# Dilated attention in a two-block network: scores in a PSUM place of their own, gate products held between blocks, bias tiles made a group ahead

## The chip, the cores and the metric

The kernel runs on one core of a Trainium2 chip. The metric is the device time of one execution in microseconds. TensorE (matrix products), VectorE, ScalarE, GpSimd and the DMA queues work side by side; each runs its own instructions in a fixed order, and they wait for each other by semaphores. The order is laid down when the program is built: the builder goes through the traced instructions and gives each engine, among those that are ready by its own estimate, the one that it ranks first. A note "issue after X" adds an edge in issue order only: the instruction is put behind X on X's engine, with no wait for X to end.

## The reference, cut to what matters

A first block (gated linear recurrence, window attention, convolution GLU) feeds a second block, which normalises x to xn and runs four mixers on a projection of it: pooling, dilated attention, stick-breaking attention and a state space layer (S5). Each mixer's output is projected and multiplied with its own gate, and the sum goes on to a feed-forward layer:

```python
for bi, yb in enumerate((y_pool, y_dil, y_sb, y_s5)):
    gate = jax.nn.sigmoid(xn @ w_gate[l, bi])
    merged = merged + gate * (yb @ w_branch[l, row:row + width])
```

The gates hang on xn alone, so they can be computed at any time after the norm. The change is about dilated attention. Twelve heads of 64 stand in three groups of four, with dilations 1, 4 and 16. A group's queries see the keys of their band, with a relative bias by a table:

```python
s = jnp.einsum('bdhnqe,bdhnke->bdhnqk', qb, kb) / math.sqrt(E)
s = jnp.where(mask, s + bias, -1e30)
m = jnp.max(s, axis=-1, keepdims=True)
p = jnp.exp(s - m)
den = jnp.sum(p, axis=-1, keepdims=True)
o = jnp.einsum('bdhnqk,bdhnke->bdhnqe', p, vb) / den
lse = (m + jnp.log(den))[..., 0]
```

The three groups' outputs are then weighed by a softmax over their `lse`. The sequence has 1024 tokens, the model width is 1024, everything is float32.

## The kernel before

Second block, in program order: stick-breaking attention (`stick`, L1737), dilated attention (`dilated`, L1838), S5 (L2028), merge (L2377). Wide products are split in a high and a low part, hi·hi + lo·hi + hi·lo, which is three matmuls for one (`gemm`, L354).

**Gates.** 32 gate tiles (four mixers by eight column tiles of 128) are to be made. `fill` (L304) takes the next one off a list: `gate` (L2359) loads 512 KB of weights, splits them (ScalarE and VectorE, L386 and L387), runs the product against the split xn (8 row tiles, 3 products, 2 halves: 48 matmuls of 512 columns, L362, L364, L366) in a PSUM tile of two banks, lets ScalarE write the tanh to `gf`, and stores that to memory as `gd`. `fill` stands at chosen places of the mixers, so that TensorE has work while a mixer's chain waits: six gates in `stick`, in `dilated` after blocks 1, 4 and 6 of each group (`FILL`, L40) and one after the third group's statistics, sixteen in S5. Only that last one of `dilated` is held by an edge (L1965); the others may be put wherever the builder finds them ready.

**PSUM.** There are eight banks. Two tiles of two banks each, `mm0` and `mm1`, are handed out in turn by `pmm` (L288), or by number. Four tiles of one bank, `ax`, come from `pax` (L292).

**Dilated attention, per group** (L1853). First the bias: one-hot tables are loaded, a small product with the bias table gives four rows (L1860), a mask is added (L1861), the rows are stored to memory (L1862) and loaded back four times as a Toeplitz tile `hk`, two buffers (L1867); a product with a reversed identity turns each (L1869), and VectorE copies it out as `bias` (L1871). Then the values: group 0 makes them by a projection (L1886), groups 1 and 2 load a transposed form and turn it with TensorE (`turn`, L1900, L1902), between the loads of q and k (L1908). Then eight blocks of 128 queries (L1913):

1. scores, four heads in two `ax` tiles (L1926). A block that sees its predecessor's keys is "wide" (256 keys), the others are "narrow" (128): group 0 has one narrow block (0), group 1 narrow blocks at even places, group 2 only narrow ones;
2. VectorE adds the bias and takes the maximum of each head (L1929), and negates it (L1932);
3. ScalarE takes the exponentials and their sums, a head at a time (L1934);
4. TensorE transposes them, four heads to an `ax` tile (L1939); ScalarE and VectorE copy them out (L1942, L1944);
5. the values product in one `ax` tile (L1951), copied to the group's result (L1954, L1956).

After the blocks, maxima and sums are transposed (L1963) and, for groups 1 and 2, reordered through memory (L1973, L1979). After the third group, the weights of the groups are computed on VectorE and ScalarE, spread (L2007, L2018) and applied (L2019, L2021).

Of the kernel before, what the change touches and what calls it, by code (L numbers as in the profile page):

```python
# [9 lines left out]
F32 = mybir.dt.float32  # L10
# [8 lines left out]
P = 128  # L19
D = 1024  # L20
T = 1024
HT = 512
# [237 lines left out]
class Kern:  # L260
# [40 lines left out]
        return self.smalls[:, o + j : o + j + 1]  # L301


    def fill(self, fp, bufs=1, turn=None, raw=False):  # L304
        if self.todo:
            b, m = self.todo.pop(0)
            g = fp.tile([P, T], F32, tag="gf", name=self.nm("gf"), bufs=bufs) if fp else self.big("gf")
            self.gate(g, b, m, turn, raw)
            if raw:
                self.raw.add((b, m))  # L310
            self.gd[b, m] = self.spill("gd", g)
# [1526 lines left out]
    def dilated(self):  # L1838
        nc, tc, A = self.nc, self.tc, self.A
        ID = self.c("ident")  # L1840
        out = []
        with tc.tile_pool(name="dl", bufs=1) as fp:
# [7 lines left out]
            ED = self.dp.tile([12, 384], F32, name=self.nm("ED"), tag="ED")  # L1850
            SD = self.dp.tile([3, 2, 32, P], F32, name=self.nm("SD"), tag="SD")
            num, stat = [], []
            for g, dil in enumerate((1, 4, 8)):  # L1853

                oh = fp.tile([32, 384], F32, tag="oh", name=self.nm("oh"))
                ng = fp.tile([4, 384], F32, tag="ng", name=self.nm("ng"))
                nc.sync.dma_start(oh, A["dil_oh"][g])
# [5 lines left out]
                bias = []  # L1863
                for h in range(4):
                    hk = fp.tile([P, 256], F32, tag="hk", name=self.nm("hk"), bufs=2)
                    e = ED[4 * g + h, :]
                    nc.sync.dma_start(hk, bass.AP(e.tensor, e.offset, [[1, P], [1, 256]]))  # L1867
                    pb = self.pax(256)
                    nc.tensor.matmul(pb, lhsT=self.c("rev"), rhs=hk, start=True, stop=True)  # L1869
                    t = fp.tile([P, 256], F32, tag="bias", name=self.nm("bias"), bufs=4)  # L1870
                    nc.vector.tensor_copy(t, pb)  # L1871
                    bias.append(t)
                if g == 0:
                    nat = lambda x, n: x[:, n * P : (n + 1) * P]
                elif g == 1:
                    nat = lambda x, n: x[:, (n % 2) * 512 + n // 2 : (n % 2) * 512 + 512 : 4]
                else:
                    nat = lambda x, n: x[:, n:T:8]
# [9 lines left out]
                else:  # L1888

                    for m in range(2):  # L1890
                        t = self.big("dvf")
# [3 lines left out]
                def turn(m):  # L1895
                    for i in range(2):
                        pp = self.pax()
                        for b in range(4):
                            c = (4 * i + b) * P
                            nc.tensor.transpose(pp[:, b * P : (b + 1) * P], vf[m][:, c : c + P], ID)  # L1900
                        o = vt[i].rearrange("p (b c) -> p b c", b=4)[:, :, m * P : (m + 1) * P]
                        nc.vector.tensor_copy(o, pp.rearrange("p (b c) -> p b c", b=4))  # L1902


                q, k = [], []
                for m in range(4):
                    t = self.big("dq" if m < 2 else "dk")
                    nc.sync.dma_start(t, self.dqd[4 * g + m])  # L1908
                    (q if m < 2 else k).append(t)
                    if vf and m in (1, 2):  # L1910
                        turn(m - 1)
                nt = [fp.tile([P, T], F32, name=self.nm("num")), self.big("num")]
                for n in range(8):  # L1913
                    prev = n > 0 if g == 0 else (n % 2 == 1 if g == 1 else False)
                    k0, c0 = ((n - 1) * P, 0) if prev else (n * P, P)
                    W = 256 - c0
                    sl = slice(n * P, (n + 1) * P)
                    s4 = fp.tile([P, 4, 256], F32, tag="ds", name=self.nm("ds"), bufs=2)
                    m4, d4 = mst[:, g, 0, :, n], mst[:, g, 1, :, n]
                    nm = self.small(4, "nm")  # L1920

                    pr = [self.pax(), self.pax()]
                    for j in range(2):
                        for r in range(2):
                            hp = slice(64 * r, 64 * r + 64)
                            nc.tensor.matmul(pr[r][:, j * 256 : j * 256 + W], lhsT=q[j][hp, sl], rhs=k[j][hp, k0 : (n + 1) * P], start=True, stop=True)  # L1926
                    for h in range(4):
                        j, r = divmod(h, 2)
                        nc.vector.tensor_tensor_reduce(  # L1929
                            s4[:, h, c0:256], pr[r][:, j * 256 : j * 256 + W], bias[h][:, c0:256], 1.0, -3e38, ALU.add, ALU.max, m4[:, h : h + 1]  # L1930
                        )
                    nc.vector.tensor_scalar(nm, m4, -1.0, None, ALU.mult)  # L1932
                    for h in range(4):
                        nc.scalar.activation(s4[:, h, c0:256], s4[:, h, c0:256], AF.Exp, bias=nm[:, h : h + 1], accum_out=d4[:, h : h + 1])  # L1934
                    pt = []
                    for c in range(c0, 256, P):
                        pp = self.pax()
                        for h in range(4):
                            nc.tensor.transpose(pp[:, h * P : (h + 1) * P], s4[:, h, c : c + P], ID)  # L1939
                        t = self.sm.tile([P, 512], F32, tag="it" if c else "dt", name=self.nm("dpt"), bufs=2)  # L1940
                        if c:
                            nc.scalar.activation(t, pp, AF.Copy)  # L1942
                        else:
                            nc.vector.tensor_copy(t, pp)  # L1944
                        pt.append(t)
                    pv = self.pax(256)
                    for h in range(4):
                        o = pv[64 * (h % 2) : 64 * (h % 2) + 64, (h // 2) * P : (h // 2 + 1) * P]
                        for i, t in enumerate(pt):
                            vb = vs[n - len(pt) + 1 + i]  # L1950
                            nc.tensor.matmul(o, lhsT=vb[:, 64 * h : 64 * h + 64], rhs=t[:, h * P : (h + 1) * P], start=i == 0, stop=i == len(pt) - 1)  # L1951
                    for j in range(2):
                        if j:
                            nc.scalar.activation(nat(nt[j], n), pv[:, P : 2 * P], AF.Copy)  # L1954
                        else:
                            nc.vector.tensor_copy(nat(nt[j], n), pv[:, 0:P])  # L1956
                    if n in FILL[g]:
                        self.fill(fp)
                num.append(nt)

                pt = self.pax(256)
                for i in range(2):
                    last = nc.tensor.transpose(pt[0:32, i * P : (i + 1) * P], mst[:, g, i].rearrange("p h n -> p (h n)"), ID)  # L1963
                if g == 2:
                    with tc.issue_after(last.ins):  # L1965
                        self.fill(fp)
                st = fp.tile([32, 256], F32, tag="st", name=self.nm("st"), bufs=3)
                if g == 0:
                    nc.vector.tensor_copy(st, pt[0:32, :])
                else:  # L1970
# [4 lines left out]
                    r = P // dil  # L1975
# [35 lines left out]
            for j in range(2):  # L2011
                y = None
                for g in range(3):
                    x = num[g][j]
                    for c in range(2):
                        ps, sl = self.pax(), slice(c * HT, (c + 1) * HT)
# [339 lines left out]
            yield  # L2356


    def gate(self, g, b, m, turn=None, raw=False):  # L2359
        hi, lo = self.load_w(self.A["w_gate"][b, m], D)  # L2360
        pg = self.pmm(turn)
        self.gemm(hi, lo, self.xtargets(pg, self.xh2, self.xl2))
        self.nc.scalar.activation(g, pg, AF.Copy if raw else AF.Tanh, scale=0.5)  # L2363


# [129 lines left out]
```

## Time and profile before

| | |
|---|---|
| median of 3 runs | 3506.52 us (3502.93 to 3508.86) |
| profiled execution | 3502.51 us |
| its span | 3500.1 us |
| TensorE busy in the span | 3308.0 us (95%) |
| VectorE, ScalarE, GpSimd busy | 62%, 40%, 21% |
| dilated attention, first score to last statistics | 1953 to 2158 us of the span |

The trace is of one execution. Times in rows are microseconds from the start of the span. A row of the timeline gives start, duration, engine, line, operation, output and input, and in brackets the idle time ahead of it and what ended it. The duration of a matmul includes its way through the engine, so that rows overlap; the rate is seen in the starts. In windows, "PEclk" is the share of the full 2.4 GHz that TensorE was granted. A float32 matmul counts as two instructions, one of a split product as one.

### The profile page before, as it was taken

To read this page: it belongs to the slowest core of one execution; us is meant where nothing else is said; L and a number is where in the kernel's file an instruction comes from. 1 tells how busy PE (TensorE), PEld (TensorE's weight loads), DVE (VectorE), ACT (ScalarE), POOL (GpSimd) and SP (SyncE) were. 2 spreads that over 40 slices of the span, in tenths; PEclk is the share of its full clock that TensorE was granted. 3 is DMA by queue.
4 is the path that set the end of the run, shared out by engine and by line. 5 is a ranking of instruction groups with operands and counts; after the bars stand their busy time and mean duration, and the time that the engine had idled before them with its cause. 6 is when DMAs were issued, how large, how long until landed. Compare 5 with 4: busy or idle time off the path is not lost. (4 is left out here: it accounts for less than half of the span.)

```text
span 3500.1 us, 42902 instructions
## 1 busy us (share of the span) xinstructions
PE 3308.0 (95%) x15531; PEld 2626.0 (75%) x15531; DVE 2170.9 (62%) x4063; ACT 1393.2 (40%) x2610; POOL 727.0 (21%) x566
## 2 busy tenths in 40 slices
PE   6999998989999999899999997999999989999998
PEld 4797776768887777688777764977778768888777
DVE  8746786685555897843377234576466674444796
ACT  5224655444444334435465333222232343333332
POOL 3200000242221532522000000223033142221440
PEclk9999999999999999999999995999999999999999
DMA  6555113322222424443321230322364422223322
GB/s 237 191 157 174 37 58 115 115 91 85 79 85 76 141 92 137 141 162 97 100 85 58 96 104 26 100 93 96 128 248 151 160 91 79 85 79 121 102 91 78
DMA packets 172019, 388.46 MB, mean 111 GB/s; under 512 B 30856, under 2 KB 61984, under 8 KB 171808
## 3 DMA queue, kind: packets, MB, share of 16 engines
q1 hardware_dynamic: 171808, 385.74, 32.4%
q8 instruction: 122, 2.00, 0.2%
q14 instruction: 89, 0.73, 0.1%
HBM read 290.59 MB, written 95.08 MB: 110 GB/s over the span
## 5 line engine op out<-in xcount | busy, mean ns | idle before, releaser
L386 ACT ACTIVATE wh<-w 128x512 fp32r<-128x512 f32 (+1 forms) x494 | 299.4, 610 | 869.1 <-PE mm L364 570.8
L362 PE MATMUL mm<-bh,wh 128*128 128x512 f32 x1544 | 599.4, 400 | 31.1 <-ACT a L909 9.0
L366 PE MATMUL mm<-bh,wl 128*128 128x512 f32 x1544 | 589.3, 396 | 4.3 <-DVE wl L387 4.3
L364 PE MATMUL mm<-bl,wh 128*128 128x512 f32 x1544 | 593.0, 396 | 0.2 <-DVE bl L387 0.2
L387 DVE TENSOR_TENSOR wl<-w,wh 128x512 fp32r<-128x512 f32 (+1 forms) x494 | 359.9, 733 | 357.3 <-ACT wh L386 338.2
L362 PEld LDWEIGHTS mm<-bh,wh 128*128 128x128 f32 x1544 | 291.7, 189 | 123.1 <-ACT a L909 11.9
L366 PEld LDWEIGHTS mm<-bh,wl 128*128 128x128 f32 x1544 | 291.1, 189 | 76.4 <-DVE wl L387 7.9
L364 PEld LDWEIGHTS mm<-bl,wh 128*128 128x128 f32 x1544 | 291.7, 189 | 65.2 <-DVE bl L387 0.9
L901 POOL TENSOR_TENSOR ws<-w 128x512 f32<-128x512 f32 x58 | 87.1, 1502 | 949.8 <-DVE rt L404 446.6
L386 ACT ACTIVATE wh<-ws 128x512 fp32r<-128x512 f32 x232 | 146.0, 630 | 270.1 <-PE mm L364 204.4
L387 DVE TENSOR_TENSOR wl<-ws,wh 128x512 fp32r<-128x512 f32 x232 | 179.4, 776 | 70.1 <-ACT wh L386 70.0
L362 PE MATMUL mm<-xh,wh 128*128 128x512 f32 x616 | 214.1, 406 | 4.2 <-ACT gf L2363 2.0
L364 PE MATMUL mm<-xl,wh 128*128 128x512 f32 x616 | 213.9, 407 | 0.0
L366 PE MATMUL mm<-xh,wl 128*128 128x512 f32 x616 | 210.7, 403 | 0.0
L366 PE MATMUL ax<-bh,wl 128*128 128x512 f32 x416 | 165.6, 398 | 4.2 <-DVE wl L387 4.2
L364 PE MATMUL ax<-bl,wh 128*128 128x512 f32 x416 | 166.2, 400 | 2.2 <-DVE bl L387 2.1
L362 PE MATMUL ax<-bh,wh 128*128 128x512 f32 x416 | 165.7, 398 | 1.6 <-ACT bh L386 1.6
L362 PEld LDWEIGHTS mm<-xh,wh 128*128 128x128 f32 x616 | 116.2, 191 | 32.7 <-issue 2.6
L364 PEld LDWEIGHTS mm<-xl,wh 128*128 128x128 f32 x616 | 116.2, 191 | 29.3 <-issue 6.1
L366 PEld LDWEIGHTS mm<-xh,wl 128*128 128x128 f32 x616 | 116.1, 191 | 27.4 <-issue 3.2
L901 POOL TENSOR_TENSOR ws<-ws,w 128x512 f32<-128x512 f32 x58 | 78.0, 1345 | 203.7 <-DMA w<-in_w_up_dram 152.3
L1563 DVE SCALAR_TENSOR_TENSOR x<-mm,adaT,x 128x512 f32<-128x512 f32 (+1 forms) x104 | 85.4, 828 | 38.4 <-PE mm L366 38.0
(637 smaller groups left out, 7153.2 us busy)
## 6 DMA issues: line engine op xcount, KB each, us to landing
w<-in_w_up_dram SPq DMA_DIRECT2D x88, 512.0 KB
wa<-in_w_ada_dram SPq DMA_DIRECT2D x64, 512.0 KB
w<-in_w_out_dram SPq DMA_DIRECT2D x32, 512.0 KB
w<-in_w_gate_dram SPq DMA_DIRECT2D x32, 512.0 KB
gd<-gf SPq DMA_DIRECT2D x32, 512.0 KB
g<-gd SPq DMA_DIRECT2D x32, 512.0 KB
y<-y SPq DMA_DIRECT2D x28, 512.0 KB
w<-in_w_down_dram SPq DMA_DIRECT2D x24, 512.0 KB
```

The costliest lines, as they stand in the source:

```text
L362: nc.tensor.matmul(ps, lhsT=wh, rhs=xh[k], start=s, stop=False, **kw)
L364: nc.tensor.matmul(ps, lhsT=wh, rhs=xl[k], start=False, stop=False, **kw)
L366: nc.tensor.matmul(ps, lhsT=wl, rhs=xh[k], start=False, stop=e, **kw)
L386: first = nc.scalar.activation(hi, src, AF.Copy)
L387: nc.vector.tensor_tensor(lo, src, hi.bitcast(F32), ALU.subtract)
L901: nc.gpsimd.tensor_tensor(t, x, y, op)
L1563: add = lambda m, x, ps: nc.vector.scalar_tensor_tensor(x, ps, self.adaT[:, 40 + m : 41 + m], x, ALU.mult, ALU.add)
```

## The change

- `fill` and `gate` take an instruction `after`; the gate's PSUM tile and matmuls are then traced with an issue-after edge to it. The weight load and its split are not held.
- In `dilated`, the fills after blocks 1, 4 and 6 pass the last score matmul of their block, and all of them use the PSUM tile `mm1`. The last fill does so behind the statistics, as before.
- Scores are written to the two banks of `mm0` instead of two `ax` tiles.
- The making of the bias tiles becomes a function: group 0's are made at the start, those of groups 1 and 2 after block 3 of the group before. There are eight bias buffers instead of four; the third group's first result tile moves to the general tiles (`big`) instead.

```diff
-    def fill(self, fp, bufs=1, turn=None, raw=False):
+    def fill(self, fp, bufs=1, turn=None, raw=False, after=None):
...
-            self.gate(g, b, m, turn, raw)
+            self.gate(g, b, m, turn, raw, after)
...
-            for g, dil in enumerate((1, 4, 8)):
-
+
+
+            def toeplitz(g):
...
-                    t = fp.tile([P, 256], F32, tag="bias", name=self.nm("bias"), bufs=4)
+                    t = fp.tile([P, 256], F32, tag="bias", name=self.nm("bias"), bufs=8)
                     nc.vector.tensor_copy(t, pb)
                     bias.append(t)
+                return bias
+
+            bias1 = toeplitz(0)
+            for g, dil in enumerate((1, 4, 8)):
+                bias = bias1
...
-                nt = [fp.tile([P, T], F32, name=self.nm("num")), self.big("num")]
+                nt = [fp.tile([P, T], F32, name=self.nm("num")) if g < 2 else self.big("num"), self.big("num")]
...
-                    pr = [self.pax(), self.pax()]
+                    pr = self.pmm(0)
+                    pr = [pr[:, 0:HT], pr[:, HT:T]]
...
-                            nc.tensor.matmul(pr[r][:, j * 256 : j * 256 + W], lhsT=q[j][hp, sl], rhs=k[j][hp, k0 : (n + 1) * P], start=True, stop=True)
+                            last = nc.tensor.matmul(pr[r][:, j * 256 : j * 256 + W], lhsT=q[j][hp, sl], rhs=k[j][hp, k0 : (n + 1) * P], start=True, stop=True)
...
                     if n in FILL[g]:
-                        self.fill(fp)
+                        self.fill(fp, turn=1, after=last.ins)
+                    if n == 3 and g < 2:
+                        bias1 = toeplitz(g + 1)
...
                 if g == 2:
-                    with tc.issue_after(last.ins):
-                        self.fill(fp)
+                    self.fill(fp, turn=1, after=last.ins)
...
-    def gate(self, g, b, m, turn=None, raw=False):
+    def gate(self, g, b, m, turn=None, raw=False, after=None):
         hi, lo = self.load_w(self.A["w_gate"][b, m], D)
-        pg = self.pmm(turn)
-        self.gemm(hi, lo, self.xtargets(pg, self.xh2, self.xl2))
+        with self.tc.issue_after(after) if after else ExitStack():
+            pg = self.pmm(turn)
+            self.gemm(hi, lo, self.xtargets(pg, self.xh2, self.xl2))
```

## Rows read from the trace of the kernel before

**Rows 1.** The page, busy time: engine, us (share of the span), instructions.

```profile
PE 3308.0 (95%) x15531; PEld 2626.0 (75%) x15531; DVE 2170.9 (62%) x4063; ACT 1393.2 (40%) x2610; POOL 727.0 (21%) x566
```

**Rows 2.** Windows by stage of dilated attention: stretch, length, busy time by engine, granted clock.

```profile
core 0: us, PE busy (x) PEld busy (x) DVE busy (x) ACT busy (x) POOL busy (x), PEclk, DMA share, GB/s
...
1916.80:1953.40 36.60, 34.42 (x240) 31.16 (x239) 2.94 (x6) 3.33 (x8) 0.00 (x0) 1.00 0.35 109
1953.40:2015.50 62.10, 59.34 (x377) 41.74 (x376) 23.87 (x93) 31.58 (x91) 0.00 (x0) 0.97 0.26 94
...
2033.00:2086.60 53.60, 53.60 (x345) 38.17 (x344) 19.94 (x89) 27.92 (x87) 0.00 (x0) 1.00 0.29 99
2086.60:2106.30 19.70, 14.03 (x55) 10.48 (x54) 5.24 (x11) 1.42 (x2) 0.00 (x0) 0.84 0.36 110
2106.30:2158.00 51.70, 30.85 (x162) 18.71 (x162) 12.27 (x81) 20.80 (x79) 0.00 (x0) 0.53 0.00 0
```

**Rows 3.** Timeline of TensorE, third group: transposes of one block.

```profile
2122.07 1.63 PE L1939 MATMUL ax<-const,ds 128*128 128x128 f32 x4 [1.92 <-ACT ds L1934]
```

**Rows 4.** Timeline of TensorE, end of the attention stage before: scores and gates.

```profile
1877.61 0.39 PE L1784 MATMUL ax<-sqh,sqh 128*128 128x512 f32 x1
...
1885.30 0.63 PE L366 MATMUL mm<-xh,wl 128*128 128x512 f32 x2
1885.77 0.22 PE L1784 MATMUL ax<-sqh,sqh 128*128 128x128 f32 x1
...
1889.03 0.71 PE L362 MATMUL mm<-xh,wh 128*128 128x512 f32 x2
```

**Rows 5.** Timeline of TensorE: first score, start of group 1, last statistics.

```profile
1953.46 0.72 PE L1926 MATMUL ax<-dk,dq 64*128 64x128 f32 x8
...
2015.76 0.80 PE L1860 MATMUL ax<-oh,tab 32*4 32x384 f32 x2
...
2028.45 1.91 PE L1900 MATMUL ax<-const,dvf 128*128 128x128 f32 x16
2030.12 0.71 PE L362 MATMUL mm<-xh,wh 128*128 128x512 f32 x2
...
2033.07 0.49 PE L1926 MATMUL ax<-dk,dq 64*128 64x128 f32 x4
...
2157.99 0.61 PE L1963 MATMUL ax<-const,mst 128*32 128x128 f32 x2
```

**Rows 6.** Timeline of TensorE, a dense run of gate matmuls: its first and tenth pair.

```profile
2017.07 0.63 PE L362 MATMUL mm<-xh,wh 128*128 128x512 f32 x2
...
2021.71 0.62 PE L364 MATMUL mm<-xl,wh 128*128 128x512 f32 x2
```

**Rows 7.** Timeline of TensorE: a wide block of group 0, a narrow one of group 1.

```profile
1993.10 1.13 PE L1926 MATMUL ax<-dk,dq 64*128 64x256 f32 x8
1994.16 0.50 PE L362 MATMUL mm<-xh,wh 128*128 128x512 f32 x1
...
1999.46 1.14 PE L1951 MATMUL ax<-dpt,vd 128*64 128x128 f32 x16
2000.53 1.13 PE L1926 MATMUL ax<-dk,dq 64*128 64x256 f32 x8
...
2047.62 0.71 PE L1926 MATMUL ax<-dk,dq 64*128 64x128 f32 x8
2048.27 0.73 PE L364 MATMUL mm<-xl,wh 128*128 128x512 f32 x2
...
2053.08 1.14 PE L1926 MATMUL ax<-dk,dq 64*128 64x256 f32 x8
```

**Rows 8.** Timeline of ScalarE: first exponentials of the two blocks of rows 7.

```profile
1996.03 0.51 ACT L1934 ACTIVATE ds<-ds,nm 128x256 f32<-128x256 f32 x1 [2.22 <-DVE nm L1932]
...
2049.60 0.40 ACT L1934 ACTIVATE ds<-ds,nm 128x128 f32<-128x128 f32 x1
```

**Rows 9.** Timeline of TensorE: the third group's v transposes.

```profile
2102.82 3.62 PE L1900 MATMUL ax<-const,dvf 128*128 128x128 f32 x16
```

**Rows 10.** Timeline of SP's queue: the last k loads of group 1.

```profile
2024.17 1.40 SPq L1908 DMA_DIRECT2D dk<-dqd x2
```

## The prediction

> **What bounds the kernel now.** I read the page's busy times first: TensorE is busy for 95% of the span [rows 1], so only places where it waits, or runs at its lower clock, can give time back. The windows by stage then show where the dilated stage has such places. Read the columns TensorE busy and granted clock. Groups 0 and 1 are full (59.34 of 62.1 us, 53.6 of 53.6), because gate matmuls run in every wait of a block. The third group's eight blocks are not: 30.85 busy of 51.7 us at a clock of 0.53 (1.2 GHz nearly throughout), and the stretch ahead of them is short of work too (14.03 of 19.7) [rows 2]. Inside that group each block waits 1.92 us for its exponentials, and in its timeline no gate matmul stands between the blocks [rows 3]. The reason stands in the timeline: the first gate of this stage starts at 1889.03, inside the attention stage before [rows 4]. The gates have run ahead of their places, and all nine have ended before the third group's blocks.
>
> So before, from the first score of group 0 (1953.46) to the third group's statistics (2157.99) [rows 5], 204.5 us pass. The change moves gates into that stretch; both ends I take as fixed and argue below.
>
> **Work that must fit between them.** One gate is 8 x 6 matmuls of 512 columns. In a dense run ten pairs start 4.64 us apart, from 2017.07 to 2021.71, so with the pair at the end 20 matmuls take 4.64 us: 0.232 each, 11.1 us a gate [rows 6]. A wide block (two key blocks): scores 1994.16 - 1993.10 = 1.06, values 2000.53 - 1999.46 = 1.07; sixteen transposes take 2030.12 - 2028.45 = 1.67, so its eight 0.83; 2.96 in all. A narrow block: scores 2048.27 - 2047.62 = 0.65, of the other two about half (0.42 and 0.59); 1.66 in all [rows 5, 7]. There are 7 + 4 = 11 wide and 1 + 4 + 8 = 13 narrow ones: 32.6 + 21.6 = 54.2 us. Add for two groups the bias (one-hot matmul 0.8, and eight passes of 256 columns at some 0.17, an estimate between a gate matmul's 0.232 and half of it: 2.1), the v transposes (1.67) and a pair of statistics (0.61 at 1.2 GHz, so 0.3) [rows 5]: 62.4 us.
>
> **Gates held.** Before, about 90 of the 96 matmuls of the first two gates stand between 1889.03 and 1953.46 [rows 4, 5]. Held behind the scores of block 1 they cannot: 20.9 us of matmuls move into the stretch. It then holds all nine gates, 100.2 us, where it held 7.1 gates, some 79.
>
> What they leave behind: the last 27 us of the attention stage and the wait for group 0's bias lose their filler. The stretch up to 1953.4 is 34.42 busy of 36.6 us [rows 2]; without gates its wait of 13 us for the bias is bare. I take the first score as not moved: the bias waits for transfers, not for gates. The bounds are -2 us (bias matmuls stand behind gate matmuls now) and +2 us (the v projections would start at 1.2 GHz).
>
> The order among ready instructions decides how well gates fill. The timeline of the attention stage shows it: the first half's last scores end by 1878, the second half's first score, whose operands are long there, starts at 1885.77, right behind the last matmul pair of a gate that the program traces ahead of it (1885.30) [rows 4]. So a gate goes ahead of whatever is traced after it. Before, gates had run so far ahead that each was traced after the current block, and gave way. Held, each is traced before the next block: it fills the waits of its own and older blocks, and then runs as a burst while the next block waits. Blocks 2, 3, 5 and 7 of a group are left with little to hide them.
>
> **Scores in their own place.** That is what the second edit buys. Until now the next scores stand behind the values of the block before (1999.46, then 2000.53) [rows 7]. With a place of their own they can start as soon as VectorE has read the last ones: the first exponential stands 2.93 us behind a wide block's score and 1.98 behind a narrow one's [rows 7, 8], so some 2.8 and 2.0 us, against 7.4 and 5.5 from one block's scores to the next's now (2000.53 - 1993.10, 2053.08 - 2047.62). The trace of before has no such overlap; the bounds of a bare pair are these two. I take the lower, since ScalarE's and VectorE's work of a block is under 3 us.
>
> Waits of TensorE that are left, by group 0, 1, 2:
> - Start, score 0 to score 1: 2.0 - 0.65 = 1.35, once.
> - After the gate of block 1: scores 2, 3 and 4 at 0, 2.8, 5.6, then the next gate is let go; 6.66 us less 3 x 1.06 and 0.83 of transposes: 2.65. Group 1 2.7, group 2 2.3.
> - After the gate of block 4: score 5 to score 6, partly covered by block 4: 0.6, 1.4, 1.35.
> - At the joins, after the gate of block 6: block 7 runs bare, 7.4 us, then statistics and v transposes (2.0), score 0 of the next group, 2.0 us later its score 1, about 1 us long. That is 12.1 us, of which 6.2 are work: 5.9, twice. The end of group 2: 5.5 - 1.66 = 3.8.
> Together 28 us.
>
> **Bias a group ahead.** The chain from the one-hot matmul to the last bias matmul takes 2028.45 - 2015.76 = 12.7 us [rows 5]. Now it sits between blocks 3 and 4, and the transposes of block 4 stand behind it for a place in PSUM (before, ready v transposes stood behind it too). Its cover: the gate of block 4 (11.1), with the rest of blocks 2 and 3, 16 us or so of work from score 4 on, against 3.5 + 12.7. I cost it at nothing; if transfers take 3 us more, 3 us, twice. The eight bias buffers and the moved result tile cost nothing on an engine.
>
> **Clock and switching.** In the third group now the v transposes behind 5 us of waiting take 3.62 instead of 1.91 us [rows 5, 9]. A join would cost at 1.2 GHz, at most, another 1.07 + 0.3 + 1.67 + 0.65 = 3.7 us; two cost 0 to 7.4, I take 5. Alternation between gate and block matmuls: in the wide block of rows 7, 7.43 us hold 17 gate matmuls and 2.96 us of block, so 0.5 over, 1.4 for a gate; a gate that runs half of it as a burst costs half of that: 6 us for nine.
>
> **Sum.** 62.4 + 100.2 + 28 + 5 + 6 = 201.6 us, against 204.5: -2.9. What follows waits for the statistics to come by transfer and then for VectorE; it shifts along unchanged. The profiled execution took 3502.51 us, 2.4 around its span of 3500.1, and 4.0 less than the median of 3506.52; put to the median, 3503.6.
>
> The Trainium skill (Trainium Kernel Development and Optimization, Best Practices) says that matmul busy time is a poor measure of headroom, and the weight load's share a better one. Group 1 shows 38.17 of 53.6 for it; by that rule 29% of groups 0 and 1 would be room, and the moved gates free (rival 4). The steady 0.232 us a matmul speaks for the opposite.
>
> **Rivals.**
> 1. Gates give way after all. Then only the start and the end of the stage wait, 5 of the 28 us, and the clock stays up: -2.9 - 23 - 5 = -31 at best; with half of that left, -17: 3490. For it: groups 0 and 1 now, full to the last us. Against: the order at 1885 [rows 4].
> 2. The joins overlap: score 0 of the next group starts inside block 7 (its tiles are there), and the clock stays up. Saves 2 x 3.5 + 5: -15, 3491. Against: the v transposes and last k load are traced in between.
> 3. Slower: the k tiles come late. Before, the last k loads were issued at 2024.17, and group 1's first score came at 2033.07 [rows 5, 10], 8.9 us later, under gates. If the held program issues them only behind the v transposes of a join, their 9 us lie bare there, less the 2 to 3 of transposes and statistics, with the clock at 1.2 GHz: +6 twice: +9, 3516. It decides from the point where the load is issued after block 7's scores. For it: the loads stand behind the gate's store in SP's queue. Against: that store is done before block 7.
> 4. Room inside the dense stretches: 0.29 x (62.1 + 53.6) = 33 us would take the 20.9: -24, 3483. Rows 6 speak against it.
> 5. Scores don't run ahead (a wait keeps them behind the values): blocks 2 and 3 at 7.4 each add 6 us a group, the rest 3: +27, 3530.
>
> **Chances.** Forecast 0.42, rivals 0.15, 0.15, 0.19, 0.03, 0.06. About 0.2%, 7 us, is what a measurement of this kernel can tell. The forecast's own range is -11 to +6 (clock 0 to 7.4, first score -2 to +2, bubbles a third off). Faster by more: rivals 1, 2 and 4 and a tail of the forecast, 0.40; slower: most of rival 3, rival 5, a little of the forecast, 0.21; within: 0.39. Range 3482 to 3517.
>
> **What would show it.** Right: no gate matmul ahead of block 1's score in group 0; the third group's blocks with three gates and a clock near 1; bursts of gate matmuls with the next score right behind; joins of 10 to 13 us at part clock; the wait for group 0's bias bare; the first score near 1953. Wrong: gate matmuls spread over blocks 2, 3, 5, 7 (rival 1); score 0 of a group ahead of the values of block 7 (rival 2); that score waiting for a transfer (rival 3); a stretch from first score to last statistics off 202 by over 8 us.

## The result, and the profile after

The changed kernel takes 3532.03 us (median of 4 runs, 3529.09 to 3533.43), the kernel before 3507.69 us in the same session: ratio 1.0070, 95% interval 1.0052 to 1.0087. It is 24 us slower. The forecast was 3503.6 us with a range up to 3517.

The page: TensorE has 18 us more busy time than before [rows 1], with the same number of instructions.

```profile
PE 3326.4 (94%) x15531; PEld 2638.3 (75%) x15531; DVE 2172.4 (62%) x4063; ACT 1392.7 (39%) x2610; POOL 728.5 (21%) x566
```

The profiled spans differ by 30.3 us (3530.4 and 3500.1), and the two timelines say where. At the last gate of the attention stage, ahead of all changed code, the changed kernel is already late: that gate's last pair starts at 1891.01, before at 1885.30 [rows 4]. These 5.7 us arise in parts of the program that the change does not touch (0.6 us at 100 us, 5.5 at 700). The medians are 24.3 us apart, so they have little room for them. Behind the stage nothing moves: S5's first product (L1727) follows the last statistics by 25.7 us in both. So the loss lies in the stretch that the forecast named, from the first score (1959.78) to the third group's statistics (2186.97): 227.19 us, against 204.53 before [rows 5]; forecast 201.6.

Windows of the changed kernel: the attention tail, the wait for group 0's bias, some gaps between gates, and the whole stretch. Columns as in [rows 2].

```profile
core 0: us, PE busy (x) PEld busy (x) DVE busy (x) ACT busy (x) POOL busy (x), PEclk, DMA share, GB/s
1889.00:1920.90 31.90, 24.46 (x88) 14.12 (x86) 25.49 (x55) 20.00 (x39) 0.00 (x0) 1.00 0.18 55
1920.90:1935.70 14.80, 5.31 (x10) 2.31 (x11) 1.97 (x5) 0.00 (x0) 0.00 (x0) 0.50 0.56 169
...
1964.30:1978.60 14.30, 14.30 (x82) 10.93 (x81) 3.51 (x13) 4.71 (x14) 0.00 (x0) 1.00 0.00 0
1978.60:1993.80 15.20, 12.86 (x55) 7.59 (x55) 4.87 (x22) 7.49 (x21) 0.00 (x0) 0.63 0.20 70
...
2110.10:2128.90 18.80, 12.14 (x68) 8.91 (x67) 8.06 (x27) 5.98 (x20) 0.00 (x0) 0.74 0.37 116
...
1959.78:2186.97 227.19, 199.97 (x1101) 142.37 (x1100) 69.20 (x287) 85.08 (x266) 0.00 (x0) 0.92 0.20 64
```

A gate's stretch (1964.30 on) is full. The gap behind it is 15.20 us long at a clock of 0.63, a join 18.80 us at 0.74. The whole stretch has 27.2 us without a matmul (227.19 - 199.97).

TensorE's timeline around block 2 of group 0 and around the join to group 1 (L362 to L366 gates, L1933 scores, L1946 transposes, L1958 values, L1972 statistics, L1906 v transposes):

```profile
1978.05 0.63 PE L366 MATMUL mm<-xh,wl 128*128 128x512 f32 x2
1978.60 1.13 PE L1933 MATMUL mm<-dk,dq 64*128 64x256 f32 x8
1981.31 0.70 PE L1933 MATMUL mm<-dk,dq 64*128 64x256 f32 x4 [1.57 <-DVE mst L1936]
...
1984.85 1.22 PE L1933 MATMUL mm<-dk,dq 64*128 64x256 f32 x2
...
1987.26 2.15 PE L1958 MATMUL ax<-dpt,vd 128*64 128x128 f32 x16 [0.57 <-DVE dpt L1951]
1989.34 2.07 PE L1933 MATMUL mm<-dk,dq 64*128 64x256 f32 x6
...
1993.87 0.78 PE L362 MATMUL mm<-xh,wh 128*128 128x512 f32 x1
...
2033.44 0.62 PE L364 MATMUL mm<-xl,wh 128*128 128x512 f32 x2
2033.91 0.63 PE L366 MATMUL mm<-xh,wl 128*128 128x512 f32 x2
2034.46 1.14 PE L1933 MATMUL mm<-dk,dq 64*128 64x256 f32 x8
2038.06 1.92 PE L1946 MATMUL ax<-const,ds 128*128 128x128 f32 x8 [2.46 <-ACT ds L1941]
2040.65 2.05 PE L1958 MATMUL ax<-dpt,vd 128*64 128x128 f32 x16 [0.68 <-DVE dpt L1951]
2042.63 0.61 PE L1972 MATMUL ax<-const,mst 128*32 128x128 f32 x2
2043.03 2.32 PE L1906 MATMUL ax<-const,dvf 128*128 128x128 f32 x16
2045.29 0.71 PE L1933 MATMUL mm<-dk,dq 64*128 64x128 f32 x8
2047.46 0.70 PE L1933 MATMUL mm<-dk,dq 64*128 64x256 f32 x4 [1.46 <-DVE mst L1936]
...
2050.22 0.71 PE L362 MATMUL mm<-xh,wh 128*128 128x512 f32 x2
...
2123.87 0.49 PE L1933 MATMUL mm<-dk,dq 64*128 64x128 f32 x4 [1.50 <-DMA dk<-dqd]
2125.19 0.49 PE L1933 MATMUL mm<-dk,dq 64*128 64x128 f32 x4 [0.82 <-DMA dk<-dqd]
```

The pattern is the forecast one: a gate runs as a burst, the next score stands right behind it, and then blocks run bare. The size is not. Score 2 to the next gate takes 15.3 us where 6.7 was forecast: score 3 comes 2.71 us behind score 2, as said, but score 4 only 8.0 us behind score 3, behind the values of block 2, and most of it runs at half clock (1.2 GHz; the values take 2.08 instead of 1.07 us [rows 7]). At the second join the k tiles are late by 1.50 + 0.82 us, a piece of rival 3.

### The profile page after: what moved, and what is told of

Same layout as the page of the kernel before. It is cut to its first block, busy times and chain, and to the rows that moved or that the text cites. A ratio compares the mean times of both kernels' runs of the same rounds, so it can differ in the third digit from the quotient of the medians.

```text
span 3530.4 us, 42891 instructions
## 1 busy us (share of the span) xinstructions
PE 3326.4 (94%) x15531; PEld 2638.3 (75%) x15531; DVE 2172.4 (62%) x4063; ACT 1392.7 (39%) x2610; POOL 728.5 (21%) x566
## 5 line engine op out<-in xcount | busy, mean ns | idle before, releaser
L362 PE MATMUL mm<-bh,wh 128*128 128x512 f32 x1544 | 599.3, 400 | 32.5 <-ACT a L909 9.0
L366 PE MATMUL mm<-bh,wl 128*128 128x512 f32 x1544 | 589.4, 396 | 4.7 <-DVE wl L387 4.6
L362 PEld LDWEIGHTS mm<-bh,wh 128*128 128x128 f32 x1544 | 291.4, 189 | 124.9 <-DVE x L2445 12.7
L366 PEld LDWEIGHTS mm<-bh,wl 128*128 128x128 f32 x1544 | 291.6, 189 | 77.1 <-DVE wl L387 8.4
L362 PE MATMUL mm<-xh,wh 128*128 128x512 f32 x616 | 213.7, 407 | 2.7 <-DVE x L1563 1.8
L366 PE MATMUL mm<-xh,wl 128*128 128x512 f32 x616 | 209.9, 403 | 0.0
L366 PE MATMUL ax<-bh,wl 128*128 128x512 f32 x416 | 165.5, 398 | 4.2 <-DVE wl L387 4.2
L362 PE MATMUL ax<-bh,wh 128*128 128x512 f32 x416 | 165.1, 397 | 1.6 <-ACT bh L386 1.6
L362 PEld LDWEIGHTS mm<-xh,wh 128*128 128x128 f32 x616 | 117.1, 192 | 30.9 <-issue 2.5
L366 PEld LDWEIGHTS mm<-xh,wl 128*128 128x128 f32 x616 | 116.5, 191 | 27.7 <-issue 2.9
```

The source lines that it names most:

```text
L362: nc.tensor.matmul(ps, lhsT=wh, rhs=xh[k], start=s, stop=False, **kw)
L366: nc.tensor.matmul(ps, lhsT=wl, rhs=xh[k], start=False, stop=e, **kw)
```

## The experiments

Each starts from one of the two kernels, or from an experiment before it. The diffs show the lines that matter; `...` marks lines left out. The stretch is first score to third group's statistics in the kernel's own trace, which is of one execution; idle is its length less TensorE busy, and the clock is the mean granted over it. For the kernel before, the row of that window is:

```profile
1953.46:2157.99 204.53, 174.41 (x1012) 121.58 (x1011) 68.13 (x285) 84.17 (x263) 0.00 (x0) 0.86 0.23 78
```


| kernel | ratio to before (95%) | median, us | before, us | stretch, us | idle, us | clock |
|---|---|---|---|---|---|---|
| before | | | | 204.5 | 30.1 | 0.86 |
| after | 1.0070 (1.0052 to 1.0087) | 3532.0 | 3507.7 | 227.2 | 27.2 | 0.92 |
| e1_hold | 1.0236 (1.0218 to 1.0254) | 3589.7 | 3508.3 | 286.3 | 62.2 | 0.77 |
| e2_place | 0.9933 (0.9919 to 0.9948) | 3483.8 | 3508.3 | 177.2 | 9.7 | 0.99 |
| e3_bias | 0.9999 (0.9989 to 1.0010) | 3504.9 | 3508.3 | 206.1 | 30.1 | 0.85 |
| e4_nohold | 0.9927 (0.9910 to 0.9945) | 3480.0 | 3508.3 | 174.4 | 7.9 | 1.00 |
| e5_late | 0.9976 (0.9968 to 0.9984) | 3498.7 | 3506.5 | 195.7 | 7.6 | 1.00 |
| e6_mix | 0.9921 (0.9907 to 0.9934) | 3479.0 | 3506.5 | 173.5 | 3.6 | 1.00 |
| e7_two_free | 1.0014 (1.0004 to 1.0023) | 3511.7 | 3506.5 | 204.2 | 25.4 | 0.92 |
| e8_hold_place | 1.0146 (1.0130 to 1.0162) | 3557.7 | 3506.5 | 249.0 | 41.7 | 0.86 |
| e9_warm | 1.0057 (1.0044 to 1.0069) | 3529.4 | 3510.1 | 226.9 | 15.6 | 0.96 |
| e10_end | 0.9909 (0.9892 to 0.9926) | 3475.6 | 3510.1 | 173.7 | 3.7 | 1.00 |
| e11_mix_ax | 1.0005 (0.9996 to 1.0014) | 3511.3 | 3510.1 | 206.8 | 29.3 | 0.89 |
| e12_whole | 0.9937 (0.9923 to 0.9951) | 3487.7 | 3510.1 | 187.3 | 14.8 | 0.93 |

### Which part costs: e1 to e4

**e1_hold**, the kernel before and the hold alone:

```diff
...
-                        self.fill(fp)
+                        self.fill(fp, after=last.ins)
...
```

> The kernel before with only the hold: gates issued behind the score of their block, scores still in two ax tiles, bias made where it was. Theory H (holding is what costs: the attention tail and group 0's bias wait lose 21 us of gate matmuls, and each held gate ends in a burst behind which the next blocks run bare): 14 bare blocks of 5.5 to 7.4 us, two bare bias chains of 12.7 us and nine gates give some 250 to 265 us for the stretch first score to last statistics, +45 to +60 us against before. Rival P (the scores' single place costs): the hold alone is within 10 us of before. Rival B (the bias in the middle of a group costs): the same.

Measured: 81 us slower by the medians. The direction is theory H's, the size beyond it. With scores in `ax`, the blocks between two gates run bare: 62.2 us idle, at a mean clock of 0.77:

```profile
1956.12:2242.41 286.29, 224.06 (x1101) 158.16 (x1100) 69.81 (x287) 87.22 (x266) 0.00 (x0) 0.77 0.16 51
```

**e2_place**, the kernel before and the scores' place alone:

```diff
-                    pr = [self.pax(), self.pax()]
+                    pr = self.pmm(0)
+                    pr = [pr[:, 0:HT], pr[:, HT:T]]
...
-                        self.fill(fp)
+                        self.fill(fp, turn=1)
...
```

> The kernel before with only the scores' place: scores in mm0, all gates of the stage in mm1, nothing held, bias where it was. Theory H: faster than before, by 15 to 35 us: with one place only, gates go out one after another, about two still run in the attention tail, and the third group's blocks get some; no stretch longer than 3 us without a matmul in the blocks. Rival P: slower by 10 us or more. Rival B: no change within 7 us.

Measured: 24.5 us faster. Rivals P and B are out. The edit also puts all gates of the stage in one PSUM tile; no run separates that from the scores' place here (e11 takes away the scores' place alone, beside held gates).

**e3_bias**, the changed kernel with the other two edits undone:

```diff
-                    pr = self.pmm(0)
-                    pr = [pr[:, 0:HT], pr[:, HT:T]]
+                    pr = [self.pax(), self.pax()]
...
-                        self.fill(fp, turn=1, after=last.ins)
+                        self.fill(fp)
...
```

> The changed kernel with the hold and the scores' place undone: only the bias tiles are made a group ahead. Theory H: faster than before by 3 to 10 us, as the third group's bias no longer stands bare ahead of its blocks; the third group's eight blocks stay bare, some 50 us. Rival B: slower by 5 us or more. Rival P: within 7 us of before.

Measured: no difference. Theory H's 3 to 10 us did not come, nor rival B's loss.

**e4_nohold**: the changed kernel without the hold.

```diff
-                        self.fill(fp, turn=1, after=last.ins)
+                        self.fill(fp, turn=1)
```

> The changed kernel without the hold of its nine gates between blocks (scores in mm0, gates in mm1, bias a group ahead). Theory H: faster than before by 20 to 40 us, so 45 to 65 us faster than the changed kernel. Rivals P and B: still slower than before by 10 us or more.

Measured: 28 us faster than before by the medians, ratio 0.9927. One argument, `after`, is the whole loss: in the stretch 174.4 against 227.2 us.

```profile
1960.60:2135.01 174.41, 166.49 (x1018) 116.44 (x1017) 66.38 (x284) 80.31 (x261) 0.00 (x0) 1.00 0.24 80
```

### What the hold costs: e5 to e7

**e5_late** keeps the hold, but traces each gate some blocks later, so that it ranks behind them:

```diff
...
+                LATE = {3: [0], 5: [3], 7: [5], 11: [7], 13: [11], 15: [13], 19: [15], 21: [19], 23: [21]}
...
-                    if n in FILL[g]:
-                        self.fill(fp, turn=1, after=last.ins)
+                    lasts.append(last.ins)
+                    for r in LATE.get(8 * g + n, ()):
+                        self.fill(fp, turn=1, after=lasts[r])
```

> The changed kernel, all nine gates still held, but each traced two to four blocks behind the score that lets it go, so that it ranks behind the work of those blocks. Theory H in two parts: the move of 20.9 us of gate matmuls out of the attention tail, and the bursts (rank ahead of the next block). With the bursts gone and the move kept, the stretch should be that of the kernel without the hold plus the moved matmuls, 174.4 + 20.9 = 195 us (changed kernel: 227), so 12 us faster to 3 us slower than before. Rival M (only the move and the bare tail cost, rank does not matter): 18 to 27 us slower than before, as the changed kernel.

Measured: stretch 195.73 us, 8 us faster than before.

```profile
1960.22:2155.95 195.73, 188.14 (x1101) 131.91 (x1101) 68.54 (x288) 83.95 (x266) 0.00 (x0) 1.00 0.22 71
```

This row stands against the last row of the changed kernel's windows: the same 1101 instructions in 31.5 us less. 19.6 of it is waiting (27.2 to 7.6), 11.8 is busy time (199.97 to 188.14) at a clock of 1.00 instead of 0.92. That is the price of rank, with one reservation: the edges, too, stand one block earlier than in the changed kernel, two of them two blocks, and no run separates the two.

**e6_mix**: as e5, but the first two gates free and traced after block 1, and seven held late, at other blocks than in e5:

```diff
...
+                LATE = {5: [2], 7: [5], 11: [7], 14: [11], 16: [14], 20: [16], 23: [20]}
...
+                    if g == 0 and n == 1:
+                        self.fill(fp, turn=1)
+                        self.fill(fp, turn=1)
...
```

> The changed kernel with the first two gates free, as before, and the seven others held but traced late. Theory H: within 6 us of the kernel without any hold (26 us faster than before), since that one leaves TensorE only 8 us idle between first score and last statistics; a better spread can give 5 us at most. Rival M: the same. If holding by itself costs something, 10 us or more behind it.

Measured: stretch 173.53 us with 3.6 us idle. e5 less e6 is 22.2 us: 18.2 of busy time, since 83 gate matmuls fewer stand in the stretch, and 4.0 of waiting. As the late gates stand at other places too, this is not the price of the two gates alone; e7 gives that.

```profile
1960.93:2134.46 173.53, 169.98 (x1018) 116.87 (x1018) 66.85 (x285) 79.04 (x261) 0.00 (x0) 1.00 0.24 80
```

**e7_two_free**, the changed kernel with two gates let go:

```diff
-                        self.fill(fp, turn=1, after=last.ins)
+                        self.fill(fp, turn=1, after=last.ins if 8 * g + n > 4 else None)
```

> The changed kernel with the first two gates free and the seven others held as in the change. Theory H: the 20.9 us go back to the attention tail, the bursts of seven gates stay: stretch 206 us and some 5 us more for blocks 3 to 5 of group 0, which then run bare; 0 to 8 us slower than before. Rival M: the gain is all of it, 20 to 30 us faster than before.

Measured: stretch 204.2 us, 5 us slower than before, as expected: the moved work is back in the tail, the bursts are still there. Nothing else differs from the changed kernel, so the move of two gates out of the attention tail costs 23.0 us (227.2 to 204.2).

### What the other two edits are worth: e8 and e11

**e8_hold_place**, the changed kernel with the bias made at each group's start:

```diff
...
-                bias = bias1
+                bias = toeplitz(g)
...
-                    if n == 3 and g < 2:
-                        bias1 = toeplitz(g + 1)
```

> The changed kernel with the bias tiles made at the start of their group again: hold and scores' place alone. If making them ahead is hidden under the held gates, as the forecast had it, its undoing lays two chains of 12.7 us bare at the joins, less some 3 us of bias work each that leaves the fourth gate's stretch, and about 3 us each for the lower clock: 20 to 30 us behind the changed kernel, 44 to 54 us behind before. If it is worth nothing: as the changed kernel, 24 us behind before.

Measured: 51 us behind before, 22 us of stretch behind the changed kernel. Where gates are held, making the bias ahead is worth 22 us; where they are not (e2 against e4), 3, which the times of the two do not tell apart.

**e11_mix_ax**, e6 with scores in `ax` again:

```diff
-                    pr = self.pmm(0)
-                    pr = [pr[:, 0:HT], pr[:, HT:T]]
+                    pr = [self.pax(), self.pax()]
```

> The kernel with two free and seven late gates, with scores in two ax tiles again: what the scores' place is worth once gates give way. Its order of TensorE shows scores behind the values of the block before, ten to seventeen gate matmuls in each block's waits, and no gate left for six blocks and part of a bias chain. If the place works by letting blocks overlap, so that fewer gate matmuls are needed to cover them: stretch 185 to 200 us, 10 to 25 us behind the same kernel with the place. If the gain came from the spread of the gates alone: within 5 us of it.

Measured: 33 us of stretch behind e6, more than expected, and no faster than before. So the place is worth that much where gates give way: without it the stretch waits 29.3 us instead of 3.6, with the same gate matmuls in it.

### Two terms of the sum: e9 and e12

**e9_warm**: six matmuls of 512 columns behind the scores of blocks 2, 3, 5 and 7, written to an `ax` tile that nothing reads.

```diff
+                    if n in (2, 3, 5, 7):
+                        with tc.issue_after(last.ins):
+                            pw = self.pax()
+                            for i in range(6):
+                                nc.tensor.matmul(pw, lhsT=self.xh2[0][i][:, 0:P], rhs=self.xh2[0][i], start=True, stop=True)
```

> The changed kernel with six more matmuls of 512 columns right behind the scores of blocks 2, 3, 5 and 7 of each group, into an ax tile that nobody reads: 72 of 0.232 us, 16.7 us of extra work laid into waits of 1.2 to 2.5 us. If the low clock behind the bursts carries some 12 us of the stretch's 227, it stays near 1 and the stretch falls to 212 to 222 us: 5 to 15 us faster than the changed kernel, in spite of more work. If the clock is only a companion and the order of the waits is all: 0 to 10 us slower than the changed kernel.

Measured: neither. The stretch is the same, 226.85 us.

```profile
1952.99:2179.84 226.85, 211.21 (x1173) 149.99 (x1172) 68.28 (x287) 85.30 (x266) 0.00 (x0) 0.96 0.19 64
```

By the starts of its rows the extra work takes 19.3 us. It fills 11.6 us of the waits (27.2 to 15.6), and the rest of the work shrinks by 8.1 us (211.21 - 19.3 against 199.97) as the clock goes from 0.92 to 0.96. The low clock is a real part of the price, but warming buys back only what it costs.

**e12_whole**: e6 with each block's scores put behind the last transpose of the block before:

```diff
...
+                    with tc.issue_after(lt.ins) if lt else ExitStack():
                     for j in range(2):
...
-                            nc.tensor.transpose(pp[:, h * P : (h + 1) * P], s4[:, h, c : c + P], ID)
+                            lt = nc.tensor.transpose(pp[:, h * P : (h + 1) * P], s4[:, h, c : c + P], ID)
...
```

> The kernel with two free and seven late gates, with each block's scores put behind the last transpose of the block before, so that they go out four or two at a time instead of in pieces between transposes. The stretch holds 188 us of TensorE work at full clock with nine gates where the forecast's unit prices gave 163; by the starts of its rows, scores take 30 us there where dense ones would take 20. If the pieces cost those 10 us: scores fall to 21 to 25 us, and the stretch gets shorter by that less the waits that come back (three blocks find few gate matmuls left): 165 to 175 us, 0 to 8 us faster than with pieces. If the price lies in every change between kinds of matmul, whatever the size of the piece: scores stay near 30 us and the stretch grows to 176 to 185 us.

Measured: neither. In groups 0 and 1 scores still go out in twos, gates run short, and the waits are back (14.8 us idle). The profiled execution was the slowest of the five, 10.4 us above their median, so its stretch may be longer than usual. Only the third group, where scores stay whole, tells something: 47.28 us, against 52.29 in e6. By the starts of the rows, scores take 6.0 us there instead of 8.4. Gates take 30.9 instead of 33.1, but there are nine matmuls fewer of them in this window (116 against 125), so one costs as much as in e6, 0.27 us. So whole scores are cheaper, and the gates' price did not change. The rows are e6's and e12's:

```profile
2082.17:2134.46 52.29, 51.30 (x305) 36.93 (x304) 18.17 (x91) 24.71 (x87) 0.00 (x0) 1.00 0.20 62
...
2102.69:2149.97 47.28, 45.79 (x296) 34.18 (x295) 16.69 (x90) 24.89 (x86) 0.00 (x0) 1.00 0.21 69
```

### A version that beats both: e6 and e10

**e10_end** adds to e6 one gate behind the third group's statistics, ranked behind the spreading of the weights, and so takes one from S5.

```diff
+                if j == 0:
+                    self.fill(fp, turn=1, after=last.ins)
                 self.dump(f"ydil{j}", num[0][j])
```

> The kernel with two free and seven late gates, and one more gate (taken from those that S5 makes) behind the third group's statistics, ranked behind the spreading of the group weights, where TensorE waits and runs at 0.7 of its clock. If that stretch's waits are worth filling: 3 to 8 us faster than the same kernel without it. If the gate delays the weights' matmuls, or S5 misses its filler: 0 to 6 us slower.

Measured: 0.9909 against e6's 0.9921, intervals that overlap: not told apart. Both beat before by 0.8 to 0.9%, and by their ratios to it the changed kernel by 1.5 to 1.6%. But e2 (0.9933) and e4 (0.9927) lie in overlapping intervals with e6 too: the scores' place without any hold, with gates in one tile, already has the gain, and no run shows that holding or a bias made ahead adds to it.

## Why the prediction was wrong, step by step

**Held: the frame.** The first score is not moved (1959.78, less the 5.7 us of early offset 1954.07, against 1953.46), within the bounds of 2 us. Its cover is gone as said: 14.80 us from the one-hot matmul to the v projections, 5.31 busy at half clock. What follows the statistics shifts along. The moved gates cost 23.0 us (e7), forecast 20.9. Gates rank ahead of the next block and run as bursts; rival 1 is out.

**Held: the waits.** 27.2 us idle, forecast 28. Two places show that this is not only a sum that happens to fit: 2.3 us in the gap of block 2 of group 0 (15.20 - 12.86; forecast 2.65) and 6.7 at the second join (18.80 - 12.14; forecast 5.9), though 2.3 of the latter is the late k tiles.

**Failed: "Clock and switching", and with it the sum.** The forecast put work at 62.4 + 100.2 = 162.6 us, switching at 6 and the clock at 5. e5 has the same work at full clock: 188.1 us busy. So switching, taken as all that the unit prices leave over, is 25.5 us there. From e5 to the changed kernel busy time grows by 11.8 us, at a lower clock. With the waits, 188.1 + 11.8 + 27.2 = 227.1, against 227.2 measured. So the two terms are 37.4 us together (199.97 - 162.6) and not 11, which is the whole miss of 25.6 us, with the waits at -0.8.

How the 37.4 us divide is less sharp. With e5's switching they are 25.5 and 11.8, but the changed kernel switches less often than e5. Its own trace bounds the clock's part; these are its stretches at 1.2 GHz:

```profile
1982.40:1996.10 13.70, 13.13 (x48) 8.29 (x48) 4.47 (x19) 4.66 (x17) 0.00 (x0) 0.50 0.10 39
2040.50:2043.90 3.40, 3.25 (x23) 2.86 (x24) 0.80 (x3) 0.45 (x2) 0.00 (x0) 0.50 1.01 400
2067.80:2074.60 6.80, 6.11 (x27) 3.66 (x26) 2.81 (x19) 2.88 (x12) 0.00 (x0) 0.50 0.31 115
2115.50:2122.40 6.90, 6.21 (x36) 5.21 (x34) 3.57 (x6) 1.00 (x2) 0.00 (x0) 0.51 0.27 73
2125.80:2132.60 6.80, 5.88 (x19) 4.13 (x19) 2.51 (x19) 2.93 (x14) 0.00 (x0) 0.50 0.00 1
```

They hold 34.6 us of busy time. If all of it ran half as fast as it could, the clock costs 17.3 us, which leaves 20.1 for switching. So the clock's part is 12 to 17 us (forecast 5) and switching's 20 to 25 (forecast 6): both terms were too small. The forecast looked for the low clock at the joins alone; two of the five stretches, 20.5 us of 37.6, lie between the gates of a group (1982.40 and 2067.80).

Where the switching sits in e5, by the starts of its rows: gates 113.4 us (forecast 100.2), scores 30.1 (20.1), all else 2.3 over. A wide block of group 0 in e6's timeline shows the scores' share:

```profile
1974.06 0.70 PE L1935 MATMUL mm<-dk,dq 64*128 64x256 f32 x4
1974.69 0.44 PE L1948 MATMUL ax<-const,ds 128*128 128x128 f32 x2
1975.06 0.70 PE L1935 MATMUL mm<-dk,dq 64*128 64x256 f32 x2
1975.69 0.44 PE L1948 MATMUL ax<-const,ds 128*128 128x128 f32 x2
1976.06 0.70 PE L1935 MATMUL mm<-dk,dq 64*128 64x256 f32 x2
1976.68 0.66 PE L1948 MATMUL ax<-const,ds 128*128 128x128 f32 x4
```

A single head (x2) takes 0.63 us from its start to the next, as long as two heads issued together (x4). Three pieces make 0.63 + 0.63 + 0.62 = 1.88 us of a wide block, where the whole of four heads took 1.06 [rows 7]. With a place that is freed head by head, scores go out in such pieces; the forecast took the price of a whole block from a kernel that hardly split one, and put its pieces at nothing. Whole scores in e12's third group bear this out.

The gates' share shows at the edges of a burst: the last pair takes 0.55 us to the score (2033.91 to 2034.46), the one before it 0.47. All of e5's rows say the same by their starts. The 296 gate matmuls that stand between two others take 0.231 us each, as forecast (in [rows 6], 2021.71 is the eleventh pair). The 135 next to another kind hold all the 13 us: 9.5 on the 85 next to scores, values and a few others, 0.11 each, and 3.8 on the 50 next to transposes alone. The latter is mostly a matter of where the starts fall: two transposes and a gate matmul take 0.46 us there, against 0.44 by dense prices.

The changed kernel's own rows at full clock say what the forecast left out. Its 419 gate matmuls there take 8.3 us over their dense price, not far from the 6 that were put for switching. But 161 score matmuls take 6.3 over, and 115 transposes 3.1, and both were put at nothing.

The Trainium skill (TensorEngine Tiling (Array Packing), Key Properties) says that a change of tiling mode drains TensorE. Scores are 64*128 in these rows, values 128*64, gates and transposes 128*128, so the rows agree with it. So does the change between gates and transposes, which keeps the mode and costs next to nothing. That the drain is the cause is argued, not shown.

**What would have shown it.** The sum was not put to the kernel before: 62.4 of work, 79 of gates and 30.1 of waits (the table) are 171.5 us, where 204.5 pass. The 33 us that are missing there, the third group's low clock and switching, were in the trace. The forecast's own range names the clock, the first score and the waits; switching is not in it.

**Scores' place and bias.** The place does what the forecast said where it has room (score 3 at 2.71 us, forecast 2.8), but three scores in a row do not run at that step: score 4 stands behind the values of block 2. Rival 5's time, 3530 us, was nearest (its +27 counts from the forecast, so it is 24 above before), but by luck: its wait, scores always behind values, is not what happened, and the waits are no longer than forecast. The bias chain cost TensorE 0.57 and 0.48 us of waiting, forecast nothing, and the k tiles of the second join 2.3 of the 12 us that rival 3 adds for two joins. Rival 4's room is not there: the moved gates cost 23.0 us (e7), no less than their time.

**The chances.** The forecast gave slower 0.21, nearly all of it to transfers (rival 3). A dearer sum of its own terms had hardly any, though the clock and the switching were the least known.

## What to carry to other kernels

A filler that is held with an edge and traced ahead of the work it should fill outranks that work: it runs as a burst and leaves the waits bare. Hold it if it must not run ahead, but trace it behind the work that it is to cover (e5 against after, 31.5 us), and leave free what has waits of its own to fill earlier (e7 against after, 23.0 us). Here no hold at all was as good as any (e2 and e4 against e6). A sum of unit prices is put to the kernel before first; what it fails to explain there is the size of its error.

## What the hardware showed that was not expected

Two score heads on the two halves of the array's rows take as long as one (0.63 us), so a block of four heads in three pieces takes 1.88 us, against 1.06 whole. Matmuls laid into the waits raised the clock from 0.92 to 0.96 and gave back 8.1 us of busy time, about as much as the 7.7 us of them that found no wait to fill.
